# Dense experts for blocks 0 and 1, gathered experts for blocks 2 and 3, and 32 expert products moved beside the early stages

## The chip, the cores and the metric

The kernel runs on one core of one Trainium2 chip. The metric is device time in microseconds (us). A core has TensorE (PE, with its weight loads shown as PEld), VectorE (DVE), ScalarE (ACT), GpSimd (POOL), a DMA queue that is issued from SyncE (SP) and sixteen DMA engines behind all queues. Each engine runs its own instructions in the order in which they stand in the program, and waits on semaphores for the others.

## The reference

One transformer layer over 512 tokens (four blocks of 128, called 0 to 3) with 1024 channels: latent attention and an RWKV recurrence side by side, an output projection, and then a product-key expert layer. The expert layer is what the change touches:

```
q = (hb @ w_pq); s = q . sub_keys          # per head, two halves of the query
s1, i1 = top_k(s[first half], 16);  s2, i2 = top_k(s[second half], 16)
top_s, pos = top_k(all sums s1 + s2, 16);  idx = i1 * 128 + i2 at pos
gate = softmax(top_s)
act = gelu(expert_u[idx] . hb)             # 8 heads x 16 experts a token
out = sum(gate * act * expert_v[idx])
```

There are 16384 experts, with one row of 1024 numbers each in `expert_u` and in `expert_v`. All is in float32.

## The kernel before

**Stages.** Everything up to the expert layer is cut into stages that are Python generators: `F` (front: load a block, normalise, project for the recurrence), `R` (the recurrence's chunk products), `M` (latent attention), `S` (the recurrence's scan) and `B` (back: output projection, normalisation, the query product with `w_pq`, the two top-16 searches and the routing into lists). `F`, `R`, `M` and `S` run block by block, `B` for block 0, for blocks 1 and 2 together and for block 3. A loop at the end of `layer_kernel` (L1189) takes steps from several lanes of stages by planned costs; the framework's scheduler then sets the order of each engine's instructions. That order is fixed when the program is built.

**Two ways through the experts.** For a gathered block, `experts` (L961) fetches, for each of 128 list entries, the 128 rows of `expert_u` that the tokens chose (one indirect DMA on POOL, L970, 512 KB), multiplies them with the activations on DVE (L980, the sum goes to `dots`), and 32 entries later fetches the rows of `expert_v` and adds them to `acc` on DVE (L983). So a gathered block has 256 indirect DMAs and 256 DVE instructions of 128x1024. The rows land in four buffers named `ga`, and POOL waits when all four are taken. For the dense blocks, `dense` (L1044) goes through all 128 groups of 128 experts: `up` (L1083) loads 512 KB of `expert_ut` and multiplies it with the tokens of both dense blocks, `down` (L1119) multiplies the result with a gate matrix on DVE (L1126), loads 512 KB of `expert_v` and accumulates into PSUM (L1130, L1141). The gate matrix `G` is made in two halves by `gate_half` (L1020): two DVE instructions (L1027, L1028) and eight matmuls (L1035) for eight tokens.

**Whole and split.** A dense matmul either takes float32 as it is (`u_whole`, L1095 and L1130) or is done as three matmuls on high and low halves (L1109, L1141); the halves are made by ACT (L1055) and DVE (L1056).

**Blocks.** `GATHERED = (0, 3)` and `DENSE = (1, 2)`. `dense()` begins when the pools of the early stages are closed, its 16 first `up` before the first `down`; 12 more (`KEPT`) are computed in between and put into DRAM, from which `up` takes them back.

## Time and profile before

| what | us |
|---|---|
| median of 3 runs | 1789.32 (1785.22 to 1790.51) |
| profiled execution, its own time | 1786.83 |
| its span, first to last instruction | 1784.9 |
| PE busy | 1622.3 |
| DVE busy | 1352.8 |
| ACT busy | 907.3 |
| POOL busy | 723.1 |

DMA moves 520.84 MB, of which 268.47 MB are the indirect DMAs. Busy time is the time in which an engine works on at least one instruction; register, branch and DMA-issuing instructions are not in it. A float32 matmul shows as two records, so 360 whole `up` matmuls are 720 records. The granted clock is the share of TensorE's full clock that was granted in a stretch.

### The profile page before, as it was taken

Reading aid. Unit: us, or ns where it says so; the run is one execution under the profiler, and the core shown is the slowest. Engines: PE = TensorE matmul, PEld = TensorE weight load, DVE = VectorE, ACT = ScalarE, POOL = GpSimd, SP = SyncE. Lnnn points to the kernel's source line nnn. Section 1 sums busy time; section 2 is a strip of 40 time slices with the busy share of each in tenths; the row PEclk is TensorE's granted clock in tenths of the full one; section 3 lists DMA queues with packets and bytes.
Section 4 is the critical chain, followed back from the end, with each engine's and each line's share of the span. In section 5 each row is a group of like instructions: output and inputs, shape, how many; then the busy total and the mean of one; then the engine's idle time right before and its main releaser. Section 6 shows DMA issues by size and latency. Waiting matters only on the chain. (4 is left out here: it accounts for less than half of the span.)

```text
span 1784.9 us, 31084 instructions
## 1 busy us (share of the span) xinstructions
PE 1622.3 (91%) x11143; PEld 1363.3 (76%) x11143; DVE 1352.8 (76%) x3010; ACT 907.3 (51%) x2421; POOL 723.1 (41%) x560
## 2 busy tenths in 40 slices
PE   7999998998879995789997799999989889999998
PEld 6896898877665784667995478888867778888876
DVE  3422446667775698987889789999878799999895
ACT  5645635444422622257766234444777735444444
POOL 1001100447664433555445343544555554447430
PEclk9999997995769998998998999999989999999999
DMA  8545643898789998889997799999889889999985
GB/s 276 187 139 191 237 163 111 322 313 268 262 272 329 318 313 305 287 297 331 376 328 244 284 363 355 330 348 340 313 318 324 310 306 355 373 340 333 354 280 177
DMA packets 154875, 520.84 MB, mean 292 GB/s; under 512 B 17313, under 2 KB 24097, under 8 KB 154721
## 3 DMA queue, kind: packets, MB, share of 16 engines
q0 software_dynamic: 73728, 268.47, 43.1%
q1 hardware_dynamic: 80992, 250.39, 39.3%
q8 instruction: 88, 1.44, 0.3%
q14 instruction: 67, 0.54, 0.1%
HBM read 508.96 MB, written 9.83 MB: 291 GB/s over the span
## 5 line engine op out<-in xcount | busy, mean ns | idle before, releaser
L970 POOL DMA_INDIRECT ga<-in_expert_v_dram,idx x256 | 359.0, 1402 | 366.7 <-DVE acc L983 260.9
L970 POOL DMA_INDIRECT ga<-in_expert_u_dram,idx x256 | 311.9, 1218 | 337.7 <-DVE ga L980 234.2
L983 DVE SCALAR_TENSOR_TENSOR acc<-ga,dots,acc 128x1024 f32<-128x1024 f32 x256 | 327.6, 1280 | 63.7 <-DMA ga<-in_expert_v_dram,idx 60.8
L980 DVE SCALAR_TENSOR_TENSOR ga<-ga,h 128x1024 f32<-128x1024 f32 x256 | 311.6, 1219 | 65.0 <-DMA ga<-in_expert_u_dram,idx 62.1
L1141 PE MATMUL po<-xh,t 128*128 128x512 f32 x880 | 305.2, 406 | 11.7 <-DVE t L1056 5.6
L1109 PE MATMUL ps<-dh,ul 128*128 128x256 f32 x664 | 192.7, 290 | 10.6 <-DVE ul L1056 10.0
L1055 ACT ACTIVATE xh<-v 128x512 fp32r<-128x512 f32 x220 | 136.4, 627 | 121.5 <-PE po L1141 99.7
L1109 PE MATMUL ps<-dh,uh 128*128 128x256 f32 x664 | 189.7, 286 | 6.7 <-ACT uh L1055 5.2
L1141 PEld LDWEIGHTS po<-xh,t 128*128 128x128 f32 x880 | 160.9, 192 | 44.4 <-DVE t L1056 6.8
L1141 PE MATMUL po<-xl,t 128*128 128x512 f32 x440 | 179.2, 408 | 11.1 <-DVE xl L1056 10.4
L1109 PE MATMUL ps<-dl,uh 128*128 128x256 f32 x664 | 188.7, 284 | 0.0
L1095 PE MATMUL ps<-t,u 128*128 128x256 f32 x720 | 172.5, 392 | 12.8 <-DMA u<-in_expert_ut_dram 11.1
L1056 DVE TENSOR_TENSOR xl<-v,xh 128x512 fp32r<-128x512 f32 x220 | 149.6, 688 | 36.6 <-ACT xh L1055 34.1
L1095 PEld LDWEIGHTS ps<-t,u 128*128 128x128 f32 x720 | 138.6, 197 | 36.8 <-issue 6.6
L1031 ACT ACTIVATE A<-iotap,slots 128x128 f32<-128x128 f32 x512 | 156.2, 394 | 0.0
L1035 PEld LDWEIGHTS ps<-B,A 128*128 128x128 f32 x1024 | 128.8, 200 | 23.2 <-ACT A L1032 11.9
L1109 PEld LDWEIGHTS ps<-dh,ul 128*128 128x128 f32 x664 | 127.3, 192 | 21.8 <-DVE ul L1056 16.5
L1055 ACT ACTIVATE uh<-u 128x512 fp32r<-128x512 f32 x166 | 99.7, 626 | 86.3 <-PE ps L1109 67.6
L1109 PEld LDWEIGHTS ps<-dh,uh 128*128 128x128 f32 x664 | 127.4, 192 | 16.7 <-ACT uh L1055 8.0
L1035 PE MATMUL ps<-B,A 128*128 128x64 f32 x1024 | 128.5, 281 | 10.6 <-ACT A L1032 9.4
L1109 PEld LDWEIGHTS ps<-dl,uh 128*128 128x128 f32 x664 | 127.3, 192 | 3.0 <-issue 0.2
L840 PE MATMUL ps<-h2T,wst 128*128 128x128 f32 (+1 forms) x768 | 123.5, 315 | 1.6 <-DMA wst<-in_w_pq_dram 1.6
(391 smaller groups left out, 2845.7 us busy)
## 6 DMA issues: line engine op xcount, KB each, us to landing
u<-in_expert_ut_dram SPq DMA_DIRECT2D x128, 512.0 KB
v<-in_expert_v_dram SPq DMA_DIRECT2D x128, 512.0 KB
wst<-in_w_rwkv_dram SPq DMA_DIRECT2D x56, 512.0 KB
wst<-in_w_pq_dram SPq DMA_DIRECT2D x48, 512.0 KB
wst<-in_w_o_dram SPq DMA_DIRECT2D x24, 512.0 KB
wst<-in_w_mla_dram SPq DMA_DIRECT2D x16, 336.0 KB
t<-in_x_dram SPq DMA_DIRECT2D x8, 512.0 KB
wst<-in_w_ukv_dram SPq DMA_DIRECT2D x16, 256.0 KB
```

Source lines behind the costliest of these rows:

```text
L840: mm(p[:, :nb * P], w[:, kc, :], h2T[:, kc, :], start=kc == 0, stop=kc == KC - 1)
L970: G.indirect_dma_start(out=t, out_offset=None, in_=table, in_offset=bass.IndirectOffsetOnAxis(ap=idx[:, j:j + 1], axis=0))
L980: V.scalar_tensor_tensor(u, u, 1.0, h2, op0=OP.mult, op1=OP.mult, accum_out=dots[:, j:j + 1])
L983: V.scalar_tensor_tensor(acc, row_of(expert_v, j), dots[:, j:j + 1], acc, op0=OP.mult, op1=OP.add)
L1031: act(A[:, j, :], iotap, AF.Abs, scale=-1.0, bias=i2T[:, t0 + j:t0 + j + 1])
L1035: mm(p[:, j * HALF:(j + 1) * HALF], A[:, j, :], B[:, j, :], start=True, stop=True)
L1055: act(hi, t, AF.Copy)
L1056: V.tensor_tensor(lo, t, hi, op=OP.subtract)
L1095: mm(p, u[:, kc, :], hd[kc // 2][:, kc % 2, :], start=kc == 0, stop=kc == KC - 1)
L1109: mm(p, a[:, k, :], h[:, kc, :], start=kc + i == 0, stop=kc == KC - 1 and i == 2)
L1141: mm(po[i][n], ww[:, i * P:(i + 1) * P], vv, start=e + k == 0, stop=e == P - 1 and k == 2)
```

## The change

- Blocks 0 and 1 are now the dense ones, blocks 2 and 3 the gathered ones.
- Stage `B` is split in two, `N` (join: projection and normalisation) and `Q` (query: product, searches, routing), in the order F0, F1, N(0,1), Q(0,1), N2, Q2, N3, Q3.
- A new stage `U` (`beside`) starts when N(0,1) is done: for the first 32 groups it loads `expert_ut`, multiplies it whole with the tokens, and stores the product in DRAM. `up` later loads it and applies Gelu. With the 16 groups of `KEPT`, 48 groups are taken back from DRAM, where 12 were.
- The number of whole `up` groups rises from 45 to 65 (of 128), so 63 are split where 83 were.
- The lists of the dense blocks go through DRAM (`slotd`), and blocks 1 and 2 use the `ga` buffers early (`EARLY`), where block 1 did.
- `experts` of block 2 is emitted before `dense()`, that of block 3 after it.

```
-GATHERED = (0, 3)
-DENSE = (1, 2)
-EARLY = 1
+GATHERED = (2, 3)
+DENSE = (0, 1)
+EARLY = (1, 2)
+BESIDE = 32
-FIRST, AHEAD, KEPT = 12, 16, 12
+FIRST, AHEAD, KEPT = 12, 16, 16
...
-    return e < 28 or 47 <= e - AHEAD < 64
+    return e < BESIDE + KEPT or 47 <= e - AHEAD < 64
...
+    def beside(_):
+        hd = ux.tile([P, KC, nd], F32, name="hdx")
+        nc.sync.dma_start(hd, h2d)
+        for e in range(BESIDE):
+            u = ux.tile([P, KC, P], F32, tag="ux", name=f"ux{e}", bufs=2)
+            nc.sync.dma_start(u, expert_ut[e])
+            p = bank()[:, :nd]
+            for kc in range(KC):
+                mm(p, u[:, kc, :], hd[:, kc, :], start=kc == 0, stop=kc == KC - 1)
+            t = ux.tile([P, nd], F32, tag="uy", name=f"uy{e}", bufs=2)
+            act(t, p, AF.Copy)
+            kept[e] = dp.tile([P, nd], F32, name=f"a{e}")
+            nc.sync.dma_start(kept[e], t)
+            yield
...
             if e in kept:
                 acts[e] = act_tile(e)
                 nc.sync.dma_start(acts[e], kept[e])
+                if e < BESIDE:
+                    act(acts[e], acts[e], AF.Gelu)
                 return
...
     early.close()
+    experts(GATHERED[0], *routed[GATHERED[0]])
     dense()
-    for b in GATHERED:
-        experts(b, *routed[b])
+    experts(GATHERED[1], *routed[GATHERED[1]])
```

**The first gathers, on DVE.** In the kernel before, the first row products of block 0 (L980) stand at row 376 of 2062, among the recurrence of block 1 (L353, L590, L760, L769).

```order
L980 SCALAR_TENSOR_TENSOR ga_15356,dots_15349<-ga_15356,h_15347 128x1024
L590 TENSOR_TENSOR t_3919<-t_3675,t_3572 128x8x64
L353 SCALAR_TENSOR_TENSOR pm_3545<-ps_3600,cv,pm_3545 128x128
L980 SCALAR_TENSOR_TENSOR ga_15359,dots_15349<-ga_15359,h_15347 128x1024
L760 TENSOR_TENSOR t_3402<-t_3402,gnr_3889 128x512
```

Now they are those of block 2 (L984), at row 688 of 1975, behind the last step of block 2's routing (L922) and around block 3's projection (L793).

```order
L953 TENSOR_TENSOR gate_6810<-ge_6804,gs_6807 128x128
L922 SCALAR_TENSOR_TENSOR t_6677<-pi_6620,dl_6566 128x128 x2
L922 SCALAR_TENSOR_TENSOR t_6677<-bf_6695,dl_6566 128x128 x16
L984 SCALAR_TENSOR_TENSOR ga_7671,dots_7670<-ga_7671,h_7668 128x1024
L984 SCALAR_TENSOR_TENSOR ga_7674,dots_7670<-ga_7674,h_7668 128x1024
...
L793 TENSOR_TENSOR t_7010<-t_7010,ps_7012 128x512
```

The gathers moved from the middle of the early stages to their end. Ahead of the first gate row on DVE (L1027, now L1052) stood 169 gathered row instructions and stand 42; from there to the last multiplication with the gate matrix (L1126, now L1154) 341 and 348; behind it 2 and 122.

**The first gate matmuls, on PE.** In the kernel before they (L1035) stand among the early stages: block 3's projection (L784) and the routing of block 2 (L901) follow them, and block 3's query product comes later still.

```order
L784 MATMUL ps_6636<-wst_6637,yT_4334 128x512
L901 LDWEIGHTS t_6513
L901 MATMUL ps_6533<-identb,t_6513 128x128
...
L784 MATMUL ps_6636<-wst_6645,yT_4334 128x512 x2
L1035 MATMUL ps_7447<-B_24_7434,A_24_7437 128x64 x3
L1095 MATMUL ps_7459<-t_7195,u_7457 128x256 x2
```

Now the last of the 32 products of `beside` (L1038) and all but one of the sixteen column groups of block 3's query product (L845) stand ahead of them (L1060).

```order
L1038 MATMUL ps_7378<-hdx,ux_7376 128x256 x8
L845 MATMUL ps_7393<-h2T_7094,wst_7391 128x128 x8
...
L845 MATMUL ps_7460<-h2T_7094,wst_7458 128x128 x8
L1060 MATMUL ps_8515<-B_0_8502,A_0_8505 128x64 x3
L845 MATMUL ps_7472<-h2T_7094,wst_7470 128x128 x8
L1060 MATMUL ps_8515<-B_0_8502,A_0_8505 128x64 x5
```

Behind the first gate matmul PE had 16 projection matmuls, 128 query matmuls of 128 columns and 16 key matmuls of block 3; it now has 8 query and 4 key matmuls. Ahead of it stood 12 groups of `up`; now it is the 32 of `beside`.

**The end, on DVE.** Before, the program ended on the dense blocks' last splits (L1056) and sums (L1173).

```order
L1056 TENSOR_TENSOR xl_15316<-v_15309,xh_15315 128x512
L1056 TENSOR_TENSOR xl_15326<-v_15309,xh_15325 128x512
L1173 TENSOR_TENSOR xx_15335<-xx_15335,po_8318 128x512
L1173 TENSOR_TENSOR xx_15335<-xx_15335,po_8319 128x512
L1173 TENSOR_TENSOR xx_15340<-xx_15340,po_8320 128x512
```

Now block 3's rows (L984, L987) follow the sums (L1202).

```order
L1202 TENSOR_TENSOR xx_15821<-xx_15821,po_9488 128x512
L1202 TENSOR_TENSOR xx_15821<-xx_15821,po_9489 128x512
L984 SCALAR_TENSOR_TENSOR ga_16308,dots_15835<-ga_16308,h_15833 128x1024
L987 SCALAR_TENSOR_TENSOR acc_15831<-ga_16311,dots_15835,acc_15831 128x1024
...
L1202 TENSOR_TENSOR xx_15826<-xx_15826,po_9491 128x512
L991 TENSOR_TENSOR dots_15835<-dots_15835,gate_7658 128x32
L987 SCALAR_TENSOR_TENSOR acc_15831<-ga_16317,dots_15835,acc_15831 128x1024
```

Of the 122 gathered row instructions behind the last gate multiplication, 97 stand behind the first of these sums.

## Rows read from the trace of the kernel before

**Rows 1.** The page: busy us by engine, then GB/s in 40 slices.

```profile
PE 1622.3 (91%) x11143; PEld 1363.3 (76%) x11143; DVE 1352.8 (76%) x3010; ACT 907.3 (51%) x2421; POOL 723.1 (41%) x560
...
GB/s 276 187 139 191 237 163 111 322 313 268 262 272 329 318 313 305 287 297 331 376 328 244 284 363 355 330 348 340 313 318 324 310 306 355 373 340 333 354 280 177
```

**Rows 2.** Stretches: length; busy PE, PEld, DVE, ACT, POOL; clock, DMA share, GB/s.

```profile
0.00:319.00 319.00, 299.67 (x2895) 256.51 (x2896) 127.68 (x548) 172.40 (x554) 23.82 (x29) 0.97 0.56 185
319.00:774.00 455.00, 383.58 (x2810) 313.66 (x2808) 351.21 (x920) 176.70 (x550) 237.71 (x196) 0.86 0.87 301
...
0.00:778.00 778.00, 686.59 (x5718) 573.16 (x5719) 482.49 (x1479) 350.04 (x1104) 263.81 (x226) 0.91 0.74 254
...
760.90:1732.00 971.10, 902.22 (x5290) 764.74 (x5289) 855.28 (x1525) 542.56 (x1292) 468.60 (x341) 0.97 0.91 328
```

**Rows 3.** Timeline (start, us): first gather, first gate row, last gate multiplication, last gather.

```profile
319.27 1.15 POOL L970 DMA_INDIRECT ga<-in_expert_u_dram,idx  x1 [0.18 <-issue]
...
760.89 0.67 DVE L1027 TENSOR_TENSOR B<-iotap,slots 128x512 f32<-128x512 f32 x1
...
1731.50 0.61 DVE L1126 TENSOR_TENSOR q<-q,G 128x256 f32<-128x256 f32 x1
...
1734.83 1.28 DVE L983 SCALAR_TENSOR_TENSOR acc<-ga,dots,acc 128x1024 f32<-128x1024 f32 x1
```

**Rows 4.** Groups by form, PE: count, busy us, mean ns, idle before.

```profile
L784 PE MATMUL ps<-wst,yT 128*128 128x512 f32 x128 | 59.6, 600 | 0.5 <-DVE t L788 0.5
L840 PE MATMUL ps<-h2T,wst 128*128 128x128 f32 x512 | 64.9, 282 | 0.0
L847 PE MATMUL ps<-wst,t 128*128 128x128 f32 x128 | 18.3, 281 | 0.5 <-ACT t L841 0.5
L1095 PE MATMUL ps<-t,u 128*128 128x256 f32 x720 | 172.5, 392 | 12.8 <-DMA u<-in_expert_ut_dram 11.1
```

**Rows 5.** Stretches of line L666, PE busy: early, and beside gathers.

```profile
0.00:300.00 300.00, 39.56 (x960) 0.98 0.58 194
400.00:560.00 160.00, 40.92 (x545) 0.71 0.83 281
```

**Rows 6.** Groups, DVE: splits, routing, and the two gathered row instructions.

```profile
L983 DVE SCALAR_TENSOR_TENSOR acc<-ga,dots,acc 128x1024 f32<-128x1024 f32 x256 | 327.6, 1280 | 63.7 <-DMA ga<-in_expert_v_dram,idx 60.8
L980 DVE SCALAR_TENSOR_TENSOR ga<-ga,h 128x1024 f32<-128x1024 f32 x256 | 311.6, 1219 | 65.0 <-DMA ga<-in_expert_u_dram,idx 62.1
...
L1056 DVE TENSOR_TENSOR ul<-u,uh 128x512 fp32r<-128x512 f32 x166 | 110.0, 688 | 9.0 <-ACT uh L1055 7.8 <-PE ps L1109 0.7
...
L917 DVE SCALAR_TENSOR_TENSOR t<-pi,dl 128x128 bf16<-128x128 f32 x64 | 14.5, 283 | 3.1 <-PE ps L939 3.1
```

**Rows 7.** Stretch of line L1109 (split up), PE busy and records.

```profile
720.00:1785.00 1065.00, 273.93 (x1992) 0.97 0.89 320
```

**Rows 8.** DMA: the indirect queue's packets and MB; one group of expert_ut.

```profile
q0 software_dynamic: 73728, 268.47, 43.1%
...
u<-in_expert_ut_dram SPq DMA_DIRECT2D x128, 512.0 KB
```

**Rows 9.** Two of the fullest stretches, columns as in rows 2.

```profile
850.00:900.00 50.00, 50.00 (x382) 48.12 (x380) 42.90 (x110) 36.59 (x98) 21.21 (x18) 1.00 0.99 372
1500.00:1550.00 50.00, 49.81 (x313) 44.71 (x314) 49.73 (x80) 24.30 (x49) 24.64 (x18) 1.00 0.98 361
```

**Rows 10.** Gathers on POOL: the densest stretch, and two in it (timeline).

```profile
400.00:450.00 50.00, 34.86 (x27) 0.61 0.82 267
...
412.74 1.81 POOL L970 DMA_INDIRECT ga<-in_expert_u_dram,idx  x1 [1.15 <-DVE ga L980]
...
418.40 0.94 POOL L970 DMA_INDIRECT ga<-in_expert_v_dram,idx  x1 [0.31 <-issue]
```

**Rows 11.** Group: the indirect DMAs of expert_v on POOL.

```profile
L970 POOL DMA_INDIRECT ga<-in_expert_v_dram,idx x256 | 359.0, 1402 | 366.7 <-DVE acc L983 260.9 <-issue 17.4 <-DVE ti L821 14.1
```

More of the change, by code (lines that the diff above doesn't have):

```diff
@@ L105, in layer_kernel @@
     wa = early.enter_context(tc.tile_pool(name="wa", bufs=1))
+    ux = early.enter_context(tc.tile_pool(name="ux", bufs=1))
     for n in (1, 4):
@@ L343, in rwkv_in @@
         for g, cols in (("x", (12, 13)), ("k", range(4, 8)), ("r", range(4)), ("v", range(8, 12))):
[L344 to L345 removed]
+            if b not in EARLY:
+                pm[g] = sb([P, 4, P], "pm", PM, pool=wa) if len(cols) == 4 else sb([P, 2, P], "px", 1, pool=wa)
             for i, c in enumerate(cols):
@@ L955, in route @@
         o = DENSE.index(b) * P
-        if not slots:
-            slots.extend(pools[2].tile([P, nd], F32, tag="vs_2", name=f"slots{j}", bufs=3) for j in range(3))
-        for j, dst in enumerate(slots):
-            act(dst[:, o:o + P], p[:, j * P:(j + 1) * P], AF.Copy)
+        t = med(3, P)
+        act(t, p[:, :3 * P].rearrange("p (a b) -> p a b", a=3), AF.Copy)
+        nc.sync.dma_start(slotd[:, :, o:o + P], t)
     def experts(b, idx, gate):
@@ L1009, in scan, with join @@
         yield from rwkv_scan(b, *parts.pop(b), yTs[b])
-    def back(bs):
+    def join(*bs):
         xts = yield from out_proj(bs, [yTs.pop(b) for b in bs])
@@ L1015, in back, with query @@
             yield from norm_ffn(b, xt, h2T[:, :, i * P:(i + 1) * P])
-        lists = yield from retrieve(bs, h2T)
+        parts[bs] = h2T
+    def query(*bs):
+        lists = yield from retrieve(bs, parts.pop(bs))
         for b, (tv, ti) in zip(bs, lists):
             routed[b] = yield from route(b, tv, ti)
+    kept = {}
+    def beside(_):
[12 more added lines that the diff above has]
+            yield
     def gate_half(dn, g, parts):
@@ L1061, in halves @@
                 for n in "hl"]
+        for j in range(3):
+            slots.append(pools[2].tile([P, nd], F32, tag="vs_2", name=f"slots{j}", bufs=3))
+            nc.sync.dma_start(slots[j], slotd[:, j, :])
         hd = []
@@ L1079, in act_tile @@
             return taken[0][:, i * nd:(i + 1) * nd]
-        kept = {}
         def up(e, keep=False):
@@ L1146, in dense @@
         n = nd // 8
-        rest = AHEAD - FIRST + KEPT
         for e in range(FIRST):
@@ L1150, in dense @@
         for i, _ in enumerate(gate_half(dn, 0, [whole])):
-            for e in range(FIRST + i * rest // n, FIRST + (i + 1) * rest // n):
-                up(e, e >= AHEAD)
+            for e in range(FIRST + i * (AHEAD - FIRST) // n, FIRST + (i + 1) * (AHEAD - FIRST) // n):
+                up(e)
+            for e in range(i * KEPT // n, (i + 1) * KEPT // n):
+                up(BESIDE + e, True)
         po = [[psd.tile([P, 512], F32, tag="po", name=f"po{i}{n}", bufs=2 * nt) for n in range(2)] for i in range(nt)]
@@ L1178, in layer_kernel @@
     stages = {"F": (front, 16, 32), "R": (chunks, 24, 110), "M": (latent, 46, 95), "S": (scan, 10, 28),
-              "B": (back, 42, 95)}
-    after = {"F": lambda b: [("R", b - 2), ("F", b - 1)] + ([("S", 0)] if b == 1 else []),
+              "N": (join, 11, 28), "Q": (query, 31, 67), "U": (beside, BESIDE, 8 * BESIDE)}
+    after = {"F": lambda b: [("R", b - 2), ("F", b - 1)],
              "R": lambda b: [("F", b)], "M": lambda b: [("F", b)],
-             "S": lambda b: [("R", b)], "B": lambda b: [("S", b), ("M", b)]}
+             "S": lambda b: [("R", b)], "N": lambda b: [("S", b), ("M", b)], "Q": lambda b: [("N", b)],
+             "U": lambda b: [("N", b)]}
     lanes = [[("R", (b,)) for b in range(NB)], [("M", (b,)) for b in range(NB)], [("S", (b,)) for b in range(NB)],
-             [(n, bs) for n, bs in BACK], [("F", (b,)) for b in range(2, NB)]]
+             [(n, bs) for n, bs in BACK], [("F", (b,)) for b in range(2, NB)],
+             [("U", DENSE[-1:])]]
     done = {}
```

13 lines of the change are left out of this document (6 added, 7 removed).

## The prediction

> **What bounds the kernel now.** I read the busy times first, then the stretches, then the places where the gathers begin and end. PE is busy for 1622 of 1785 us and DVE for 1353 [rows 1], but no engine is the bound from end to end. Up to 319 us PE alone is full: 299.67 of 319 us, a density of 0.94, while DVE is at 0.40 and DMA moves 185 GB/s [rows 2]. At 319.27 us the first gather starts [rows 3], and from there to 774 us DMA moves 301 GB/s, DVE is at 0.77, PE falls to 0.84 and its granted clock to 0.86 [rows 2]: the gathers of block 0 use DMA and DVE time which the early stages leave over, and cost PE something for it. From the first gate row (760.89 us) to the last gate multiplication (1731.50 us) [rows 3] everything is nearly full at once: of 971 us PE is busy 902 (0.93), DVE 855 (0.88), and DMA moves 328 GB/s [rows 2]. The reader is to see that the last gathered row is done at 1734.83 us [rows 3], when the dense part is almost done too. So gathers and dense part end together, and the 512 gathers have 1416 us to spread over. Each is 268.47 MB / 512 = 0.524 MB [rows 8] and one DVE instruction of (327.6 + 311.6) / 512 = 1.25 us [rows 6].
>
> **Step 1: the early part gets longer.** The order of the changed program puts nearly all of block 3's projection and query and all of `beside` ahead of the first gate matmul on PE. Before, PE had 686.6 us of work up to 778 us, where its first gate matmul starts [rows 2]. Added: 16 projection matmuls (32 records of 128, 59.6 us), 14.9 us; 120 query matmuls of 128 columns (240 records of 512, 64.9 us), 30.4 us; 12 key matmuls (24 records of 128, 18.3 us), 3.4 us; and 32 groups of `beside` at the price of a whole group, 172.5 us / 45 = 3.83 us, together 122.7 us. Removed: the 12 whole groups of `up` that stood there, 46.0 us [rows 4]. The sum is 812 us. The rest of the early part keeps its work; blocks only change places.
>
> Something comes back, because no gather runs beside it. Line L666, the recurrence's small matmuls, takes 39.56 / 960 = 0.041 us a record before the gathers and 40.92 / 545 = 0.075 us beside them at a clock of 0.71 [rows 5]; over its 545 records that is 18 us. The whole stretch from 319 to 774 us has 383.6 us of PE work at a clock of 0.86 [rows 2], so the clock can give back between 0 and 0.14 x 383.6 = 54 us. I take the middle, 27 us, since L666 alone has 18. That leaves 785 us. With the density of the stretch without gathers, 0.94 [rows 2], the first gate matmul starts at 835 us; the first gate row on DVE leads it by 17 us, as before (760.9 against 778), so at **818 us**. `beside` needs 32 x 0.524 MB more here, which the 185 GB/s of that stretch leave room for; its copies and stores are on ACT (172 of 319 us busy) and SP [rows 2]. SP's queue takes its loads in order, so a load of `beside` that waits for one of its two buffers holds back the weight loads behind it; that price is not in the trace of before, and lies between nothing, when PE has other work, and the gap down to the density of 0.84.
>
> That block 2's gathers are emitted ahead of the dense part does not help here: they wait for block 2's routing, which itself stands behind nearly all early work, and by the order only 42 gathered rows stand ahead of the first gate row, against 169 before. **The filling of DMA and DVE between 319 and 774 us is what the change removes**, and the 127 gathers that lost their place there go to the end.
>
> **Step 2: the dense part gets somewhat shorter.** From the first gate row to the last gate multiplication the order has 348 gathered rows against 341, so this stretch can be priced from its like before, 971 us. PE loses 48.7 us of block 3's work (step 1) and twenty split groups of `up`, 273.93 / 83 = 3.3 us each [rows 7], 66 us: 902 - 49 - 66 = 787 us, at 0.93 some 847 us. DVE loses 38 split instructions at 0.688 us (26.1 us) and 90 small ones of top-16 and routing at 0.283 us (25.5 us), and gains seven gathers (8.8 us) [rows 6]: 855.3 - 42.8 = 812 us, at its own density of 0.88 some 922 us. DMA moved 328 GB/s x 971 us = 318.5 MB [rows 2]. It loses twenty groups of `expert_ut` (10.5 MB) and block 3's weights (13 MB), and gains seven gathers (3.7 MB) and 40 transfers of 0.131 MB for the groups kept in DRAM (5.2 MB): 304 MB, at 328 GB/s 926 us. In the fullest slices DVE reaches 49.73 of 50 us, and DMA 372 GB/s [rows 9]; with these 817 us would do. So PE is no longer the first bound, and DVE and DMA come out alike at 922 to 926 us with the densities of before. They waited for PE part of that time, so I take a little less, **895 us**, between 817 and 950. The Gelu on the 32 reloaded products goes to ACT, which is at 0.56 in this stretch [rows 2] and hides it; without that cover it would cost 32 activations of 542.56 / 1292 = 0.42 us, 13 us. The lists that now go through DRAM are under 1 MB, and the `ga` buffers that block 2's front borrows are free before its routing ends, so I cost both at nothing; if not, POOL's first gathers wait, and the tail grows by as much.
>
> **Step 3: a tail that was not there.** Behind the last gate multiplication the order has 122 gathered rows, against 2 before, and the last dense work covers only 25 of them. From below: DMA at its fullest, 0.524 MB / 372 GB/s = 1.41 us a gather [rows 8, 9]; POOL's shortest issue and gap, 0.94 + 0.31 = 1.25 us [rows 10], is less. From above: the densest stretch of gathers in the trace, 27 in 50 us, 1.85 us each [rows 10], with dense weights and recurrence beside it. The tail has less beside it, so 1.7 us: 122 x 1.7 = **207 us** (172 to 226), and 3 us for the last store. POOL waits longest for DVE's `acc` rows to free a buffer (260.9 us, mostly in the dense part, where DVE's order spaces them) [rows 11]; in the tail there is nothing between two of them, so that wait shrinks.
>
> **Sum.** 818 + 895 + 207 + 3 = 1923 us of span. The profiled execution of before took 1786.8 us with a span of 1784.9, and the median is 1789.3, so 4 us more: about **1927 us**, 8% slower. A check that shares little with it: DMA moved 0.254 x 778 = 198 MB up to 778 us before, so 323 MB after it; now 304 MB of step 2 and 122 x 0.524 = 64 MB, 368 MB, which at 328 GB/s are 1122 us from 818 us on: 1940 us.
>
> **Rivals.**
>
> *The late part packs tighter.* If DVE and DMA run as in their fullest slices all the way, steps 2 and 3 are 817 and 172 us: 818 + 817 + 172 + 3 + 4 = 1814 us. For it: two slices that show it [rows 9]. Against it: with the same mix DVE averaged 0.88. Chance 0.16. The Trainium skill, page "DMA: Bandwidth & Descriptors", section "Specifications", gives 358 GB/s as one core's share of the memory and 435 GB/s as the ceiling of the DMA fabric. The highest slice here is 376 GB/s [rows 1], over the first and far under the second; at 435 the 304 MB of step 2 would be an estimated 699 us, but DVE's 812 us of work would then set that step.
>
> *Gather issue takes turns with DVE.* If each issue on POOL waits for the DVE instruction before it, a gather in the tail costs 1.25 + 0.94 + 0.31 = 2.50 us [rows 6, 10], the tail 305 us, and the whole 818 + 895 + 305 + 3 + 4 = 2025 us. For it: in the dense gather stretch the issue instructions last from 0.94 up to 1.81 us, and on average 1.4 us [rows 10, 11]. Against it: 27 gathers in 50 us is faster than this would allow. Chance 0.06. The Trainium skill, page "SBUF — State Buffer", section "SBUF: two separate sides", has such a rule: POOL cannot write the descriptors of its DMAs while DVE holds the port pair that both share. By the spacing of 1.85 us it does not hold for every instruction.
>
> *The early part is loose.* If it keeps the density of 0.84 and regains no clock, 812 / 0.84 = 967 us, less 17: 950 + 895 + 207 + 3 + 4 = 2059 us. For it: SP's order above, and routing chains on DVE. Against it: 0.94 up to 319 us with chains of the same kind. Chance 0.09.
>
> *Faster.* One mechanism: the early part, freed of gathers, ends so early that the late part's smaller work pays for the tail. With all the clock back and no gaps, (812 - 54) / 0.98 - 17 = 756 us, and steps 2 and 3 at their floors: 756 + 817 + 172 + 3 + 4 = 1752 us. It decides from a first gate row at about 790 us if both floors hold, and from 680 us if only the middle values do, which is below the 741 us that PE's work alone allows (758 less 17). Chance 0.03.
>
> **How the numbers follow.** The forecast has a chance of 0.65; its own range, with the ends of steps 1 to 3 partly together, is 1850 to 2010 us. The tight case reaches from 1780 to 1850, the last two slower ones from 2010 to 2110 us. Within 0.3% of 1789 us, about what a measurement of this kernel can tell from no change, I leave 0.01. Slower by more than 0.3% is thus 0.96, faster 0.03. The range 1830 to 2045 us leaves out half of the tight case, half of the loose one and the fast one, with a little of the rest: under 0.2.
>
> **What would show it.** In the profile after: the first gather on POOL near 760 us where it was at 319; the first gate row on DVE near 818 us; DMA under 220 GB/s before the first gather; some 895 us from that gate row to the last gate multiplication, with DVE at 0.9 and PE lower than before; then some 200 us with PE idle, gathers 1.7 us apart on POOL, and the last DVE instruction a row added to `acc`. The prediction is wrong if gathers start before 600 us, if the first gate row comes before 700 us, or if the tail after the dense sums is under 50 us.

## The result, and the profile after

The changed kernel takes 2052.39 us (median of four runs, 2046.07 to 2056.64), and the kernel before, on the same chip, 1787.27 us (1782.92 to 1790.51). The ratio is 1.148, with a 95% interval from 1.144 to 1.152. The direction was forecast, the size was not: 138 us were forecast and 265 came, 7 us above the upper end of the range. The profiled execution took 2053.33 us, with a span of 2051.0 us.

The page of the kernel after (busy us by engine, then GB/s in 40 slices), against [rows 1]:

```profile
PE 1675.4 (82%) x10983; PEld 1375.9 (67%) x10983; DVE 1335.9 (65%) x2970; ACT 896.1 (44%) x2407; POOL 707.0 (34%) x560
...
GB/s 286 217 156 161 156 56 188 95 125 175 84 75 203 210 176 373 374 273 289 310 304 330 320 324 363 317 317 316 332 285 356 365 337 370 313 332 303 279 276 256
```

The busy times hardly moved (PE +53 us, DVE -17 us) although the span grew by 266 us. So the loss is idle time, and its place is what has to be found. The GB/s row shows where DMA was left unused: in slices 2 to 15 it moves 56 to 217 GB/s, where before it had moved 262 to 329 in slices 8 to 15, once the gathers had begun.

The places of [rows 3], in the kernel after (timeline on POOL and DVE: start, us): the first gather, the first gate row, the last gate multiplication, the first of the dense sums, and the last two rows that are added to `acc`:

```profile
756.92 1.16 POOL L974 DMA_INDIRECT ga<-in_expert_u_dram,idx  x1 [45.24 <-ACT idx L957]
...
867.84 2.49 DVE L1052 TENSOR_TENSOR B<-iotap,slots 128x512 f32<-128x512 f32 x4
...
1800.26 0.62 DVE L1154 TENSOR_TENSOR q<-q,G 128x256 f32<-128x256 f32 x1
...
1856.01 1.28 DVE L1202 TENSOR_TENSOR xx<-xx,po 128x512 f32<-128x512 f32 x2
...
2044.88 2.61 DVE L987 SCALAR_TENSOR_TENSOR acc<-ga,dots,acc 128x1024 f32<-128x1024 f32 x2 [0.49 <-DMA ga<-in_expert_v_dram,idx]
```

The stretches between these places, against [rows 2] (length; busy PE, PEld, DVE, ACT, POOL with their instructions; clock, DMA share, GB/s):

```profile
0.00:757.00 757.00, 719.97 (x5954) 596.27 (x5955) 279.05 (x1223) 346.99 (x1104) 46.95 (x48) 0.95 0.49 155
757.00:868.00 111.00, 82.04 (x425) 66.59 (x424) 65.08 (x166) 22.26 (x58) 51.05 (x46) 0.88 0.98 366
868.00:1800.30 932.30, 825.26 (x4428) 681.69 (x4427) 814.04 (x1369) 504.99 (x1206) 466.06 (x348) 0.93 0.91 323
1800.30:1856.00 55.70, 47.71 (x181) 31.35 (x179) 48.95 (x75) 21.38 (x39) 25.11 (x23) 1.00 0.95 348
1856.00:2051.00 195.00, 0.40 (x2) 0.00 (x0) 128.76 (x141) 0.46 (x2) 117.83 (x97) 0.51 0.82 274
```

Length less busy time gives PE's idle time: 37 us up to the first gather, 29 up to the gate row, 107 in the dense stretch, 8 up to the sums and 195 behind them. Nearly all of the added idle time is the last line, in which PE does nothing while 97 gathers are issued one after another.

### The profile page after: what moved, and what is told of

It is laid out like the page before. It is cut to its first block, busy times and chain, and to the rows that moved or that the text cites. A ratio compares the mean times of both kernels' runs of the same rounds, so it can differ in the third digit from the quotient of the medians.

```text
span 2051.0 us, 30931 instructions
## 1 busy us (share of the span) xinstructions
PE 1675.4 (82%) x10983; PEld 1375.9 (67%) x10983; DVE 1335.9 (65%) x2970; ACT 896.1 (44%) x2407; POOL 707.0 (34%) x560
## 5 line engine op out<-in xcount | busy, mean ns | idle before, releaser
L974 POOL DMA_INDIRECT ga<-in_expert_u_dram,idx x256 | 298.6, 1166 | 318.6 <-DVE ga L984 215.0
L987 DVE SCALAR_TENSOR_TENSOR acc<-ga,dots,acc 128x1024 f32<-128x1024 f32 x256 | 328.3, 1283 | 86.0 <-DMA ga<-in_expert_v_dram,idx 80.8
L984 DVE SCALAR_TENSOR_TENSOR ga<-ga,h 128x1024 f32<-128x1024 f32 x256 | 312.7, 1223 | 99.5 <-DMA ga<-in_expert_u_dram,idx 98.5
L1169 PE MATMUL po<-xh,t 128*128 128x512 f32 x880 | 318.4, 420 | 46.8 <-ACT xh L1080 32.3
L1060 PEld LDWEIGHTS ps<-B,A 128*128 128x128 f32 x1024 | 135.2, 212 | 38.2 <-ACT A L1057 26.6
L1060 PE MATMUL ps<-B,A 128*128 128x64 f32 x1024 | 137.2, 296 | 25.2 <-ACT A L1057 21.4
L1056 ACT ACTIVATE A<-iotap,slots 128x128 f32<-128x128 f32 x512 | 156.4, 394 | 0.0
L1137 PE MATMUL ps<-dh,ul 128*128 128x256 f32 x504 | 145.6, 289 | 9.6 <-DVE ul L1081 9.5
L1137 PE MATMUL ps<-dh,uh 128*128 128x256 f32 x504 | 145.5, 289 | 3.5 <-ACT uh L1080 3.0
L1137 PE MATMUL ps<-dl,uh 128*128 128x256 f32 x504 | 144.0, 286 | 0.0
L845 PE MATMUL ps<-h2T,wst 128*128 128x128 f32 (+1 forms) x768 | 129.4, 325 | 14.1 <-DMA wst<-in_w_pq_dram 14.1
L1123 PE MATMUL ps<-t,u 128*128 128x256 f32 x528 | 135.6, 413 | 0.5 <-ACT G L1065 0.5
L845 PEld LDWEIGHTS ps<-h2T,wst 128*128 128x128 f32 x768 | 112.9, 201 | 24.1 <-issue 15.4
L1038 PE MATMUL ps<-hdx,ux 128*128 128x256 f32 x512 | 124.0, 393 | 0.1
L1123 PEld LDWEIGHTS ps<-t,u 128*128 128x128 f32 x528 | 107.6, 209 | 17.8 <-issue 0.7
L1169 PEld LDWEIGHTS po<-xl,t 128*128 128x128 f32 x440 | 86.7, 197 | 47.3 <-DVE xl L1081 31.2
```

Source lines behind the costliest of these rows:

```text
L845: mm(p[:, :nb * P], w[:, kc, :], h2T[:, kc, :], start=kc == 0, stop=kc == KC - 1)
L974: G.indirect_dma_start(out=t, out_offset=None, in_=table, in_offset=bass.IndirectOffsetOnAxis(ap=idx[:, j:j + 1], axis=0))
L984: V.scalar_tensor_tensor(u, u, 1.0, h2, op0=OP.mult, op1=OP.mult, accum_out=dots[:, j:j + 1])
L987: V.scalar_tensor_tensor(acc, row_of(expert_v, j), dots[:, j:j + 1], acc, op0=OP.mult, op1=OP.add)
L1038: mm(p, u[:, kc, :], hd[:, kc, :], start=kc == 0, stop=kc == KC - 1)
L1056: act(A[:, j, :], iotap, AF.Abs, scale=-1.0, bias=i2T[:, t0 + j:t0 + j + 1])
```

## The experiments

The theory going in was the prediction's, that the gathers lost their place beside the early stages. Open were three things: what sets the pace of the gathers (bytes, DVE, or the four `ga` buffers), whether it is the choice of blocks or `beside` that costs the time, and whether the place of the emission matters. Each experiment is an edit of the kernel after, unless it says "of before". The kernel before measured 1786 to 1788 us beside each of them.

### What sets the pace of the gathers

**Half of DVE's work per row.** The row instructions work on 512 of 1024 columns, so half of each product and of each sum is left out; the transfers stay whole.

```
-V.scalar_tensor_tensor(u, u, 1.0, h2, ...
+V.scalar_tensor_tensor(u[:, 0:512], u[:, 0:512], 1.0, h2[:, 0:512], ...
-V.scalar_tensor_tensor(acc, row_of(expert_v, j), dots[:, j:j + 1], acc, ...
+V.scalar_tensor_tensor(acc[:, 0:512], row_of(expert_v, j)[:, 0:512], dots[:, j:j + 1], acc[:, 0:512], ...
```

> Both gathered row instructions on DVE work on 512 of the 1024 columns (so the gathered blocks' result is only half computed); the indirect DMAs still fetch whole rows. Three theories on what paces the changed kernel from its first gather (757 us) on. DMA theory: the sixteen DMA engines pace it, at the 321 GB/s that it averages there; the bytes stay, so the time stays: 2010 to 2065 us, and a gathered row behind the last gate multiplication still takes 1.9 to 2.1 us. DVE theory: 512 rows at 1.25 us pace it; some 0.6 us of each goes, 300 us in all, and the time falls to 1800 to 1880 us. Buffer theory: four ga buffers and the round trip of one gather pace it; of a round trip of 4 x 2.03 = 8.1 us 0.6 us goes, so the tail falls by 7% or some 20 us and the whole to 1990 to 2030 us.

**Half of both.** The same, and each gather brings half a row, 2 KB for 4, so half of the gathered data is left out too (the halves come from other rows of the table; only their amount matters here).

```
-G.indirect_dma_start(out=t, out_offset=None, in_=table,
+G.indirect_dma_start(out=t[:, 0:512], out_offset=None, in_=table.rearrange("n (a b) -> (n a) b", a=2),
```

> As the run with half of the columns on DVE, and each indirect DMA fetches 2 KB of a row where it fetched 4 KB (other numbers, so the gathered blocks' result is not computed): 134 MB less. DMA theory: 134 MB at 0.32 MB/us are up to 420 us, until PE bounds the dense part (825 us of work behind the first gate row at 868 us, so about 1750 us); 1740 to 1820 us, far below the run with whole rows. DVE theory: no change against the run with whole rows, within 40 us. Buffer theory: the round trip loses the transfer's half, 0.5 to 1 us of 8, so 6 to 12% of the gathers' time: 1900 to 1980 us.

**Three buffers.** Block 2's early use of the buffers has to go with the fourth one.

```
-EARLY = (1, 2)
-GROUP, GA = 32, 4
+EARLY = (1,)
+GROUP, GA = 32, 3
```

> Three ga buffers where there were four; block 2's front uses its own tiles, since three buffers cannot hold two blocks' fronts. Buffer theory: a gather in the tail takes 4/3 of 2.03 us, 2.7 us, and with the 175 rows that the order now leaves behind the last gate multiplication the tail is some 470 us where it was 250; the whole 2200 to 2280 us. DMA theory: a gather in the tail stays at 2.0 to 2.2 us, DMA stays near 270 GB/s there, and only the longer tail shows, 175 x 2.1 = 370 us with a dense part 50 to 100 us shorter: 2060 to 2130 us. DVE theory: the same as the DMA theory.

Measured: 1968.17, 1853.18 and 2239.02 us, one run each. None of the theories held for the first: it lies between the ranges of the buffers and of DVE. None held for the second: it lies between those of DMA and of the buffers. The third is in the range of the buffers, but a gather in its tail took 2.34 us where that theory had 2.7. Stretches of the three (columns as above): first the dense stretch, from the first gate row to the last gate multiplication, and for the first and the third the tail behind the dense sums.

Half of DVE's work:

```profile
861.80:1753.10 891.30, 805.06 (x4429) 673.02 (x4429) 644.88 (x1367) 506.74 (x1206) 403.04 (x356) 0.94 0.95 343
...
1802.90:1966.40 163.50, 0.54 (x3) 0.10 (x1) 71.02 (x130) 0.23 (x1) 85.76 (x91) 0.52 0.88 306
```

Half of both:

```profile
861.00:1800.40 939.40, 819.85 (x4435) 681.12 (x4436) 713.23 (x1533) 511.89 (x1211) 512.95 (x454) 0.93 0.78 255
```

Three buffers:

```profile
878.10:1818.20 940.10, 830.50 (x4434) 692.77 (x4434) 763.97 (x1304) 511.14 (x1211) 390.61 (x304) 0.91 0.86 296
...
1878.40:2237.10 358.70, 1.51 (x7) 0.89 (x5) 198.37 (x223) 0.46 (x2) 157.37 (x153) 0.51 0.74 231
```

*The tail* goes at the pace of a round trip over the buffers. A gather took 195 / 97 = 2.01 us with four buffers, 358.7 / 153 = 2.34 us with three, and 163.5 / 91 = 1.80 us with four and half the DVE work. Times the number of buffers, one buffer comes round in 8.0, 7.0 and 7.2 us. The view of DMA issues gives the largest part of that, the time from the start of the issue to landing (last number, median us). In the tail of the kernel after, of the one with three buffers, and of the one with half the DVE work:

```profile
ga<-in_expert_v_dram,idx POOLq DMA_INDIRECT x65, 5.6
...
ga<-in_expert_u_dram,idx POOLq DMA_INDIRECT x32, 5.6
```

```profile
ga<-in_expert_v_dram,idx POOLq DMA_INDIRECT x93, 5.2
ga<-in_expert_u_dram,idx POOLq DMA_INDIRECT x60, 5.2
```

```profile
ga<-in_expert_v_dram,idx POOLq DMA_INDIRECT x62, 5.7
...
ga<-in_expert_u_dram,idx POOLq DMA_INDIRECT x29, 5.5
```

So of 8.0 us, 5.6 go from the start of the issue to landing, 1.26 to the row instruction on DVE, and about 1.2 to waiting for a turn on DVE and POOL. A fourth buffer makes landing slower (5.2 to 5.6 us) but still gives more gathers at a time: DMA moves 274 for 231 GB/s. Halving DVE's instruction cuts the round trip by 0.8 us: some 0.53 us of its own (1.26 to 0.73), and the rest is waiting, since landing stays at 5.5 to 5.7 us.

The issue instructions, which are a part of the landing time, become shorter too: 117.83 / 97 = 1.21 us each in the tail after, and 85.76 / 91 = 0.94 us here. The timeline of the tail after shows why:

```profile
1954.85 1.28 DVE L987 SCALAR_TENSOR_TENSOR acc<-ga,dots,acc 128x1024 f32<-128x1024 f32 x1
1955.00 1.94 POOL L974 DMA_INDIRECT ga<-in_expert_u_dram,idx  x1 [0.84 <-DMA ga<-in_expert_v_dram,idx]
...
1962.57 0.94 POOL L974 DMA_INDIRECT ga<-in_expert_u_dram,idx  x1 [0.70 <-DVE ga L984]
```

The first issue starts while a row runs on DVE, and lasts until 0.8 us after that row's end; the second starts beside no row. Of 94 issues between 1862 and 2045 us, the 47 that start during a row take 1.49 us on average, and the 47 others 0.94. With half rows 86 of 87 issues start beside no row. The rule of the Trainium skill, page "SBUF — State Buffer", section "SBUF: two separate sides", that POOL cannot write descriptors while DVE holds the port pair that both share, agrees with these times. It lengthens an issue by 0.27 us on average; the rival's full price, 2.50 us a gather, did not come, since half of the issues meet no row and other gathers are under way in the meantime.

What POOL and DVE wait for in the kernel after from 1856 us on (engine, line, waited for: us in total, times, longest) says the same from the other side. Nobody is full (DMA 0.82, DVE 0.66, POOL 0.60 of the time); each waits for the next one in the ring:

```profile
DVE acc L987 <- DMA ga<-in_expert_v_dram,idx: 42.1, 48, 1.8
POOL ga L974 <- DVE acc L987: 33.4, 31, 1.9
DVE ga L984 <- DMA ga<-in_expert_u_dram,idx: 19.0, 23, 2.1
POOL ga L974 <- DVE ga L984: 18.5, 15, 2.6
```

*The dense stretch* behaves otherwise. It lasted 932 us in the kernel after, and 939 us with 255 instead of 323 GB/s and 101 us less DVE work, but with 106 more gathers in it. With half the DVE work alone it lasted 891 us. So in that order of work the bytes don't set it, and DVE only in part; what stands in all four kernels is PE's 805 to 830 us of work and 86 to 120 us in which it waits. With half of both, the last row came at 1678 us and there was no tail: the kernel ends on the dense part, at 1851 us. That separates two ends, which the next experiments follow.

### The place of the emission

**Emission as before**, in the kernel after:

```
-    experts(GATHERED[0], *routed[GATHERED[0]])
     dense()
+    experts(GATHERED[0], *routed[GATHERED[0]])
     experts(GATHERED[1], *routed[GATHERED[1]])
```

> Block 2's expert rows are emitted behind the dense part again, as both gathered blocks were before; all else as in the changed kernel. My theory: the place of emission is without weight, since the rows wait for block 2's routing and the order still has 42 of them ahead of the first gate row and 123 behind the last gate multiplication: 2035 to 2070 us, within 1% of 2052. Rival: emission ahead of the dense part puts the gathers' DVE rows ahead of the gate rows and delays the first gate row (868 us against the 818 us forecast); then this run has its first gate row 30 to 50 us earlier and takes 2000 to 2030 us.

**Emission as after**, in the kernel before:

```
+    experts(0, *routed[0])
     dense()
-    for b in GATHERED:
-        experts(b, *routed[b])
+    experts(3, *routed[3])
```

> The kernel of before with block 0's expert rows emitted ahead of the dense part, nothing else. Theory of the two chains: nothing moves, since the order is the same but for two rows (169 rows ahead of the first gate row, 343 in the dense part, none behind): 1775 to 1800 us, within 0.7% of before. Rival (emission ahead of the dense part puts gathers before dense rows on DVE and slows the dense part): over 1810 us.

Measured: 2047.76 us (one run), with the first gather at 753.3 us and the last row starting at 2040.7 us; and 1794.69 us, ratio 1.003 (1.001 to 1.006). Both fell where expected. The place of the emission is worth some 5 us in the one kernel, no more than runs of the kernel after differ (2046 to 2057 us), and 6 in the other, of 265.

### The choice of blocks and `beside`

**Blocks as before**, `beside` kept:

```
-BACK = [("F", (0,)), ("F", (1,)), ("N", (0, 1)), ("Q", (0, 1)), ("N", (2,)), ("Q", (2,)), ("N", (3,)), ("Q", (3,))]
-GATHERED = (2, 3)
-DENSE = (0, 1)
+BACK = [("F", (0,)), ("F", (1,)), ("N", (0,)), ("Q", (0,)), ("N", (1, 2)), ("Q", (1, 2)), ("N", (3,)), ("Q", (3,))]
+GATHERED = (0, 3)
+DENSE = (1, 2)
```

> The changed kernel with the blocks of before: 0 and 3 gathered, 1 and 2 dense, N and Q for block 0, for 1 and 2, for 3; the 32 products beside, the 65 whole groups and the early emission stay. The order has 260 gathered rows ahead of the first gate row (42 in the changed kernel), 252 in the dense part and none behind it. My theory (the choice of blocks moves the first gather from 319 to 757 us, and this alone makes the tail): the first gather is back at 320 to 360 us, the tail of 250 us is gone, the first gate row comes at 860 to 930 us and the whole takes 1770 to 1850 us. Rival (the products beside and the split of the back stage cost the time): the time stays over 1950 us.

**No `beside`**, blocks as after (its lane of the loop is taken out as well):

```
-BESIDE = 32
+BESIDE = 0
```

> The changed kernel without stage U: the 32 products are computed in the dense part as the rest, 95 groups split and 33 whole. PE's early work is 123 us less and its dense work 32 x 3.3 = 106 us more. My theory (the dense part is paced by PE and by the engines' orders at a density near 0.89, so what is taken out of it early comes back late): the first gather at 620 to 680 us, a dense part of 1000 to 1070 us, a tail of 155 rows, 300 us; the whole 2010 to 2100 us, within 2.5% of the changed kernel. Rival (the products beside delay block 2's routing and so cause the slowdown): first gather at 640 us and all else as much earlier, 1930 to 1960 us.

**Blocks 0 and 1 gathered**, without `beside`, the rest as after:

```
+BACK = [("F", (0,)), ("F", (1,)), ("N", (0,)), ("Q", (0,)), ("N", (1,)), ("Q", (1,)), ("N", (2, 3)), ("Q", (2, 3))]
+GATHERED = (0, 1)
+DENSE = (2, 3)
+BESIDE = 0
```

> The other way round: blocks 0 and 1 gathered, 2 and 3 dense, each of 0 and 1 joined and queried alone, without the products beside; the rest as in the changed kernel. The order has 224 gathered rows ahead of the first gate row, 288 in the dense part, none behind it. My theory (what counts is how early gathers start and that none is left at the end): first gather at 320 to 370 us, first gate row at 760 to 830 us, no tail, 1770 to 1840 us. Rival (any block choice other than that of before leaves a tail or starves the early part): over 1900 us.

**Blocks 0 and 1 gathered, of before:**

```
-BACK = [("F", (0,)), ("F", (1,)), ("B", (0,)), ("B", (1, 2)), ("B", (3,))]
-GATHERED = (0, 3)
-DENSE = (1, 2)
+BACK = [("F", (0,)), ("F", (1,)), ("B", (0,)), ("B", (1,)), ("B", (2, 3))]
+GATHERED = (0, 1)
+DENSE = (2, 3)
```

> The kernel of before with blocks 0 and 1 gathered and 2 and 3 dense, nothing else changed. Order: 223 gathered rows ahead of the first gate row, 289 in the dense part, none behind it. My theory: gathers of block 1 fill the stretch near 1000 us in which the kernel of before waits for block 3's routing, but the dense part waits for block 3's query product: 1760 to 1820 us, within 2% of before. Rival (the earlier the gathers, the better, without limit): under 1750 us.

**Blocks as before and no `beside`**, the fourth corner: both of the first two edits.

> The changed kernel with the blocks of before (0 and 3 gathered) and without the products beside: the fourth corner to the changed kernel (2052 us), to it without the products (2023) and to it with the blocks of before (1988). What the eight runs so far suggest: the gathers need some 1300 us from the first to the last, the dense part some 1000 us from the first gate row to the end, whatever the blocks, and the time is the later of the two ends. The order has 165 gathered rows ahead of the first gate row and none at the end, as in the kernel of before (169 and 2). Theory of the two chains: first gather at 330 to 365 us, first gate row at 740 to 800 us, and 1760 to 1830 us, within 3% of before: each of the two edits alone then costs 200 us and both together 266, since they do not add but push different chains. Rival (the costs of the two edits add): 2023 + 1988 - 2052 = 1959 us. Rival (what else the change brought, the split of the back stage, 16 kept groups and the early emission, costs 200 us): 1950 us or more.

**Blocks as before and a quarter of `beside`**: `BESIDE = 8`.

> The blocks of before with 8 products beside in place of 32; 24 groups whole in the dense part, the rest as in the run with the blocks of before. Two chains: the dense part starts when the products beside are done, so with a quarter of them the first gate row lies a quarter of the way between the runs with none and with 32 of them (some 770 and 1037 us): 800 to 860 us, and the whole 1800 to 1870 us. Rival (the products beside fill idle time of PE and only too many of them hurt): the first gate row as without them, and under 1785 us.

| kernel | us | ratio (95%) | first gather | last row | first gate row | dense end |
|---|---|---|---|---|---|---|
| before | 1787 | | 319 | 1736 | 761 | 1785 |
| after: gathers 2, 3; 32 beside | 2052 | 1.148 (1.144 to 1.152) | 757 | 2047 | 868 | 1864 |
| gathers 0, 3; 32 beside | 1988 | 1.110 (1.102 to 1.118) | 350 | 1656 | 1037 | 1993 |
| gathers 2, 3; none beside | 2023 | 1.134 (1.127 to 1.140) | 705 | 2011 | 681 | 1762 |
| gathers 0, 3; none beside | 1832 | 1.027 (1.022 to 1.032) | 350 | 1761 | 789 | 1830 |
| gathers 0, 3; 8 beside | 1862 | 1.039 (1.035 to 1.043) | 351 | 1774 | 853 | 1871 |
| gathers 0, 1; none beside | 1940 | 1.085 (1.078 to 1.092) | 361 | 1706 | 941 | 1943 |
| before, gathers 0, 1 | 1896 | 1.064 (1.057 to 1.070) | 323 | 1675 | 919 | 1893 |

(The last four columns are times in the profiled execution. The dense end is the end of the dense sums, or of the span where the dense part ends last.)

My own theory for the third line, that with early gathers the kernel would come down to 1770 to 1850 us, fell, and its rival, over 1950 us, was right; the ranges for the two kernels that gather blocks 0 and 1, which ended at 1840 and 1820 us, were missed as well, by 100 and 76 us. The kernel without `beside` fell into its range, with a first gather at 705 us where 620 to 680 was expected; the one with both edits came 2 us above its range, and the one with a quarter of `beside` fell into its. In the three misses the column of the first gate row is late: 941, 919 and 1037 us. With the blocks back, the gathers end at 1656 us and everything after that is the dense part alone, which had started late. Stretches of that kernel, from the first gather to the first gate row, to the last row, and to the end:

```profile
349.90:1036.90 687.00, 507.50 (x3446) 405.82 (x3445) 490.80 (x1301) 191.38 (x548) 323.03 (x277) 0.85 0.88 306
1036.90:1655.00 618.10, 516.25 (x2554) 415.02 (x2554) 506.26 (x743) 349.15 (x889) 315.17 (x250) 0.89 0.90 319
1655.00:1984.00 329.00, 327.40 (x1967) 291.58 (x1968) 205.71 (x352) 176.05 (x344) 0.00 (x0) 0.99 0.56 180
```

The last line is the counterpart of the tail in the kernel after: PE is full, POOL has nothing, and DMA moves 180 GB/s. `beside` runs here beside gathers, and PE is busy only 507 of 687 us; the first gate row comes 10 us after the last matmul of `beside`, at 1027 us. With blocks 0 and 1 gathered and no `beside`, the last routing row of the last two blocks starts at 930.6 us, and the first gate row waits for their lists (timeline, DVE):

```profile
941.12 2.50 DVE L1052 TENSOR_TENSOR B<-iotap,slots 128x512 f32<-128x512 f32 x4 [1.35 <-DMA slots<-slotd]
```

For the kernel before with these blocks the same cause is likely, but not shown.

So two lines of work run beside each other: the gathers, from the first one to the last row, and the dense part, from the first gate row to its sums. Their lengths in the table: where the gathers end last, they take 1290 us (after) and 1306 us (gathers 2, 3 without `beside`). Where the dense part ends last, it takes 956 to 1042 us, and the gathers end before it, after 1306 to 1423 us, with time to spare. (Without `beside`, blocks 2 and 3 gathered, it takes 1081 us.) The time is the later of two ends, about the first gather + 1300 us or the first gate row + 1000 us: this gives all eight lines within 2.5%. It was read from six of these lines; the two with blocks 0 and 3 gathered and none or 8 beside were forecast by it. The change moved the first gather by 438 us (319 to 757) and the first gate row by 107 us, and thereby the end from the dense part to the gathers. That is also why its two main edits don't add: from the corner at 1832 us, the blocks alone cost 191 us and `beside` alone 156 us, but both together 220 us. What is left of the change, the corner against the kernel before, costs some 45 us.

### Late gathers alone

If this is so, the kernel before must become as slow as the kernel after, when nothing but its first gather comes late. **Late gathers, of before**: block 0's list of indices gets zero times a list of block 2, the second dense block, added to it, so that its gathers cannot start before that list is there.

```
+        if b == 0:
+            V.scalar_tensor_tensor(idx, slots[0][:, P:2 * P], 0.0, idx, op0=OP.mult, op1=OP.add)
```

> The kernel of before, in which block 0's list of experts passes one more DVE instruction that adds zero times the dense blocks' lists, so that its gathers cannot start before blocks 1 and 2 are routed; nothing else is changed. It moves the first gather alone, by data and not by blocks or products. The order has no gathered row ahead of the first gate row, 339 in the dense part and 173 behind it. Two chains: first gather at 730 to 800 us, 1300 us from there to the last gathered row, so 2040 to 2110 us, although the dense part ends as early as before or earlier, at 1700 to 1790 us. Rival (late gathers are caught up with, since the stretch from 319 to 760 us has less on DVE and DMA and the dense part starts earlier): under 1900 us.

Measured: 1991.70 us (1985.61 to 2000.66), ratio 1.115 (1.109 to 1.121). That is 48 us under the range I had given. The first gather came at 688.7 us, where I had put it at 730 to 800; from there to the last row it took 1290 us, as expected. The rival, under 1900 us, did not come. Its first gather (timeline, POOL), and its stretches from the start, from the first gather, from the last gate multiplication and from the sums:

```profile
688.71 1.16 POOL L972 DMA_INDIRECT ga<-in_expert_u_dram,idx  x1 [33.65 <-DVE idx L963]
```

```profile
0.00:689.00 689.00, 659.60 (x5763) 542.66 (x5764) 284.89 (x1233) 346.17 (x1099) 45.65 (x48) 0.98 0.48 155
689.00:1635.00 946.00, 881.57 (x5198) 755.45 (x5197) 834.68 (x1488) 533.43 (x1275) 454.20 (x343) 0.97 0.92 333
1635.00:1689.30 54.30, 48.94 (x185) 31.91 (x184) 48.81 (x74) 22.04 (x41) 28.57 (x22) 1.00 0.95 348
1689.30:1978.00 288.70, 0.55 (x3) 0.11 (x1) 190.88 (x217) 0.46 (x2) 174.85 (x148) 0.51 0.83 276
```

These lines are those of the kernel after, with the same 155 GB/s ahead and the same tail, 288.7 / 148 = 1.95 us a gather. The dense part even ended 87 us earlier than in the kernel before (1698 against 1785 us), and the kernel is 204 us slower. Late gathers are enough for 204 of the 265 us; the other parts of the change are not needed for this kind of loss. The edit moves the first gate row too, from 761 to 665 us, since the early part now has no gathers beside it (PE from the start to its first gate matmul):

```profile
0.00:697.00 697.00, 666.70 (x5793) 0.98 0.48 157
```

That is a density of 0.96 where the kernel before had 686.6 of 778 us, 0.88: the early gathers cost the dense part 96 us of start there, and saved more at the end.

A sum of delay and slack sizes it. In the kernel before, the gathers took 1736 - 319 = 1417 us and ended 49 us ahead of the end; in this kernel, without slack, they take 1290 us. So a delay of the first gather should cost nothing up to 49 + 127 = 176 us, and its full length beyond. The change delays it by 438 us: 438 - 176 = 262 us, and the span grew by 266. The sum rests on the gathers' 1290 us, which both kernels with late gathers need, and does not explain that length.

## Why the prediction was right in direction and half in size

The mechanism held: late gathers, a longer early part, and a tail in which PE has no work. What failed are three terms of the sum, each too small: step 1 by 50 us, step 2 by 37 and step 3 by 41.

**The first gather, right.** Forecast near 760 us, measured 756.92; its cause, block 2's routing behind nearly all early work, stood in the order of the program. The prediction gives no sum for the 760, so that it is this close is partly luck. Before it DMA moved 155 GB/s, under the 220 that the prediction set.

**Step 1, 818 forecast and 868 measured (+50).** PE did 804 us of work up to the first gate matmul at 873 us, where the sum was 812 before anything came back: 8 us came back and not 27 (the recurrence's small matmuls, L666 and now L671, went from 102.67 to 91.83 us). And the density of 0.94 held only up to the first gather: 719.97 of 757 us. In the 111 us from there to the gate row it was 0.74, at a granted clock of 0.88 and 366 GB/s. The step that failed took the early part as free of gathers, though the order of the program showed 42 rows ahead of the gate row; 45 gathers were issued there, and DMA was at 0.98. The two waits there that matter (engine, line, waited for: us, times, longest), DVE for rows and PE for block 3's weights:

```profile
DVE ga L984 <- DMA ga<-in_expert_u_dram,idx: 39.3, 23, 8.9
...
PE ps L845 <- DMA wst<-in_w_pq_dram: 14.1, 7, 4.5
```

DVE's lead over the gate matmul was 5 us, where 17 were taken over from before. In parts: 20 us from the work, 18 from the density (0.92 up to 873 us) and 12 from the lead make the 50.

**Step 2, 895 forecast and 932 measured (+37).** The work was forecast well: DVE 812 us (814.04 measured), DMA 304 MB (323 GB/s x 932.3 us = 301 MB); PE's 787 became 825.26, at a clock of 0.93 where 0.97 had been. DVE and DMA at their own densities of before gave 922 and 926 us. The step that failed is the one behind them, to "take a little less" because PE would no longer be waited for. PE was still waited for, and waited itself: 45 of the 107 us in which it waits lie between 1050 and 1200 us. That stretch in the kernel after, then in the kernel before, and what ACT and PE wait for in the first:

```profile
1050.00:1200.00 150.00, 104.67 (x307) 61.41 (x307) 117.57 (x182) 36.52 (x75) 76.37 (x57) 0.88 0.91 319
```

```profile
1050.00:1200.00 150.00, 145.30 (x880) 124.28 (x879) 136.68 (x227) 69.86 (x142) 63.42 (x49) 1.00 0.95 344
```

```profile
ACT xh L1080 <- DMA v<-in_expert_v_dram: 31.3, 12, 4.8
...
PE po L1169 <- ACT xh L1080: 24.5, 12, 3.6
...
PE po L1158 <- DMA v<-in_expert_v_dram: 11.5, 5, 4.0
```

Here the products come back from DRAM, so PE has almost only `down` to do (285 of its 307 matmul records are of `down`), and each group of those needs its 512 KB of `expert_v` and most its split, for which ACT waits for the same load. PE is busy for 105 of 150 us, and in the kernel before it was for 145. Moving `up` ahead took work from PE at a place where the stretch then waited for something else. Without `beside`, the dense stretch is:

```profile
681.00:1699.70 1018.70, 957.02 (x5669) 822.75 (x5667) 886.06 (x1584) 560.48 (x1338) 477.16 (x361) 0.96 0.92 331
```

So PE's work is 957 us and the stretch 1018 without it, and 825 and 932 with it: of 132 us of PE work taken away, 86 came back as time.

**Step 3, 210 forecast with the store and 251 measured (+41).** The 122 rows took 2.03 us each, (2047.5 - 1800.3) / 122, where 1.7 was taken, between 1.41 and 1.85. The upper bound was the densest 50 us of gathers in the trace of before [rows 10], and "less beside it" was to make the tail quicker than that. Both failed, and in kind. The densest piece is a best case and no bound from above: the 173 gathers issued from 319 to 761 us took 2.55 us each. And what sets the tail is a round trip that less company did not bring under 8 us. That landing takes 5.6 us with nothing else running is in no row of before, where landing times of the gathers are not given; the wait of POOL for `acc` [rows 11] was the row that pointed to the buffers, and I explained it away. In the tail of the kernel after that wait is still there, 31 times, 33.4 us.

**Sum.** 50 + 37 + 41 = 128 us, the whole miss: 1923 us of span were forecast and 2051 came. The three were treated as terms that may err both ways, and all erred the same way, and as I read it for the same reason: each assumed that work packs more tightly when it has less beside it. The check by DMA shared that assumption: 374 MB were moved from the first gate row on, at 316 instead of 328 GB/s, from 868 and not from 818 us.

**The rivals.** The tight case (1814 us) did not come, nor the faster one. The loose early part (2059 us) is nearest in time but not in cause: its first gate row is at 950 us, and the kernel's at 868. Turns between gather issue and DVE are there, but lengthen an issue in the tail by 0.27 us on average, where the rival would have had 0.94 us of issue and 0.31 of gap on top of DVE's 1.25. The argument against them from the spacing of 1.85 us was wrong: in that stretch of before [rows 10] 16 of the 27 issues start during a row and take 1.57 us on average, the 11 others 0.94, and the spacing stays below 2.50 us because the rest goes on meanwhile. The borrowed lists and buffers of block 2's front, costed at nothing, are among the edits that remain in the corner at 1832 us, 45 us above the kernel before; which part of those 45 is theirs was not tried.

**What stays open.** In two kernels the first gate row comes soon after the last matmul of `beside`, as if the dense part waited for its memory: 10 us with the blocks back, 13 us in the kernel after. With eight products beside it came 122 us after them, so there something else held it. What sets the 930 to 940 us of the dense stretch, apart from PE's work, was narrowed (not bytes, DVE in part) but not settled. More than four buffers, which would test the round trip from the other side, were not tried. No version that was run is faster than the kernel before.

## What to carry to other kernels

Where two long lines of work run beside each other, write down for each where it starts, how long it takes when nothing is spare, and its slack; the time is the later end, and a step that starts one of them later costs its delay less the slack, whatever it saves the other. A stretch with one line alone costs more than its best piece elsewhere suggests: price a lone ring of transfers by buffers and round trip (issue to landing, consumer, next issue), and take the mean spacing of a long stretch as the bound from above. When several terms are uncertain, see whether the same hope stands in all of them; then they don't offset each other.

## What the runs showed of the hardware that was not expected

- Indirect gathers of 512 KB with nothing else running moved 274 GB/s with four buffers and 231 with three, and 306 with four and half the DVE work, while a mixed stretch of the kernel after moved 366 (757 to 868 us). A lone stream of gathers did not fill DMA: its busy share was 0.82, 0.74 and 0.88.
- The issue of a gather on POOL took 0.94 us when no row instruction ran on DVE at its start, and 1.49 us on average when one did (47 each in the tail after): it lasted to 0.8 us after the row's end. The mean was 1.21 us with rows of 1024 columns and 0.94 with rows of 512, which the issues hardly met.
- The granted clock fell to 0.51 in the tail, where PE was idle: the lower of its two levels, 1.2 GHz. It cost nothing there, since PE had no work left.
